# Column means of an 8192 x 8192 matrix: the last row group in loads of 4, 4, 2 and 1 blocks, five other blocks read at the start

## The chip, the cores and the metric

One core of a Trainium2 chip runs the program. The time is device microseconds of one execution, the median of five; less is better. A profile of one execution is at hand for the kernel before. Five engines work side by side, each with its own queue of instructions: TensorE (PE in the profile, its weight loads PEld), VectorE (DVE), ScalarE (ACT), GpSimd (POOL) and SyncE (SP). SyncE and ScalarE also issue DMA transfers (SPq and ACTq), and these run on 16 DMA engines.

## The reference

```python
def setup_inputs():
    return {
        "x": np.random.randn(8192, 8192).astype(np.float32),
    }

def reference(x: np.ndarray) -> np.ndarray:
    return np.mean(x, axis=0)
```

The input is 268.4 MB of float32, the output 32 KB. Every element of x has to be read once and added once.

## The kernel before

**Tiling.** The rows are cut into G = 64 groups of P = 128 rows, one row for each partition; group g is `rows(g)`, 4 MB. The columns are cut into 16 blocks of F = 512. The on-chip buffer `bufs` has six slots of one group each: four receive loads, slot 4 (`both`) holds the sum of two groups, slot 5 (`acc`) the running sum.

**Loads.** `load` (line 75) issues a transfer on SyncE's queue and appends it to `loads`. Every second one also waits for the landing of the loads seven and eight back. The order of the queue is the order of the program: `head` (blocks 0 to 3 of group 60, 768 KB), groups 0 to 3, groups 4 and 5, `ahead` (blocks 8 to 12 of group 63, 1 MB), then a loop over g from 6 to 52 with two groups, 8 MB, in each load, then groups 54 to 59 one by one, then group 60 without the blocks of `head`, 61, 62, and group 63 in three pieces: blocks 0 to 8, 12 to 14 and 14 to 16. (Ranges of blocks are given as in the code, without their upper end.) A load into a slot waits until VectorE has read what was there.

**Sums on VectorE.** `add` (line 95) is a VectorE addition. In the loop there are two for each load: the two new groups into `both`, then `both` into `acc`. Where an addition must wait for a load and for the one before, a no-op on ScalarE or GpSimd (line 98) waits for both and VectorE waits for the no-op; which of the two engines it is goes by the number of additions so far. Groups 54 to 59 are added to `acc` one by one, of group 60 only the blocks from 3 on, of group 61 only those from 5 on. GpSimd adds blocks 13 to 16 of group 62 (line 136).

**Sums on TensorE.** What is left over, and `acc` itself, is summed over the 128 partitions by matmuls with a 128 x 32 block of ones divided by 8192 (line 169). A matmul of one block goes to one of four quarters of the array (`tile_position=(0, 32 * q)`) and leaves its sum in 32 partitions of PSUM, so four of them run side by side. In float32 each matmul is two instructions in the trace. `plan` gives the order: what stands ahead in it holds up all that follows, since TensorE takes it in order. Blocks 0 to 12 go to three banks of four blocks each (`banks`), blocks 12 to 16 in pieces of W = 256 columns to two smaller tiles (`ends`).

**The end.** ScalarE copies bank 2 into `both` (line 183) and stores it (line 186, `s2`), after the landing of `loads[-3]`; then it copies banks 0 and 1 and the first small tile. VectorE copies the second small tile to `tail` (line 201). SyncE stores banks 0 and 1 together (`s01`), ScalarE blocks 12 to 14 (`s3`), SyncE blocks 14 to 16 last. `landed` (line 70) is a no-op on SyncE that waits for DMAs; three of them stand behind the last store. Then the program closes (line 239): SyncE waits for the last landings, and all engines meet.

```python
    for lo, loaded in [(3, 3), (5, 0)]:
        row = bufs[:, (g + 2) % 4, :]
        dma = load(row[:, loaded * F:], rows(g)[:, loaded * F:])
        add(acc[:, lo * F:], acc[:, lo * F:], row[:, lo * F:], [dma])
```

Of the kernel before, what the change touches and what calls it, by code (L numbers as in the profile page):

```python
# [8 lines left out]
@with_exitstack  # L9
def kernel(  # L10
    ctx: ExitStack,
    tc: tile.TileContext,
    x: bass.AP,
    out: bass.AP,
):

    nc = tc.nc
    f32 = mybir.dt.float32
    M, N = x.shape  # L40
    P = nc.NUM_PARTITIONS
    F = 512
    W = F // 2
    WHOLE = 12
    G = M // P
    U = 6
    sync = mybir.DependencyInfo(mybir.DependencyClass.Sync, mybir.DependencyReason.DATA)

    sb = ctx.enter_context(tc.tile_pool(name="sb", bufs=1))
    psp = ctx.enter_context(tc.tile_pool(name="psum", bufs=1, space=bass.MemoryType.PSUM))  # L50

    bufs = sb.tile([P, U, N], f32, name="bufs")
    both = bufs[:, U - 2, :]
    acc = bufs[:, U - 1, :]
    ones = sb.tile([P, 32], f32, name="ones")
    ahead = sb.tile([P, 4 * F], f32, name="ahead")
    tail = sb.tile([P, W], f32, name="tail")
    warm = sb.tile([P, 32], f32, name="warm")
    nc.gpsimd.memset(ones[:], 1.0 / M)  # L59
    ready = sb.tile([P, 1], f32, name="ready")  # L60
    tc.keep_in_program_order(
        nc.gpsimd.tensor_add(out=ready[:], in0=ones[:, 0:1], in1=ones[:, 1:2]))  # L62
    banks = [psp.tile([P, F], f32, name=f"bank{b}") for b in range(3)]
    ends = [psp.tile([P, W], f32, name=f"end{e}") for e in range(2)]

    loads = []

    def landed(*inss):

        nop = tc.keep_in_program_order(nc.sync.nop()).ins  # L70
        for o in inss:
            tc.add_manual_dep(nop, o.name, sync, reason="SyncE waits")

    def load(dst, src):
        ins = tc.keep_in_program_order(nc.sync.dma_start(out=dst, in_=src)).ins  # L75
        k = len(loads)
        over = loads[k - 8:k - 6] if k >= 8 and k % 2 == 0 else []
        tc.declare_no_dep(ins, group="loads", keep=over, reason="the reader of the buffer waited")
        for o in over:
            tc.add_manual_dep(ins, o.name, sync, reason="covers the next load too")  # L80
        tc.add_to_no_dep_group("loads", ins)
        loads.append(ins)
        return ins

    def rows(g, n=1):
        return x[g * P:(g + n) * P, :]

    def load_rows(g, u, n):
        return load(bufs[:, u:u + n, :], rows(g, n).rearrange("(p j) c -> p j c", j=n))

    adds, joins = [], {}

    def add(dst, a, b, dmas):

        ins = nc.vector.tensor_add(out=dst, in0=a, in1=b).ins  # L95
        if dmas and adds:
            waiter = nc.scalar if len(adds) % 8 > 1 else nc.gpsimd
            nop = joins[waiter] = tc.keep_in_program_order(waiter.nop()).ins  # L98
            for o in dmas + adds[-1:]:
                tc.add_manual_dep(nop, o.name, sync, reason="the no-op waits")  # L100
            for group in ("loads", "adds"):
                tc.declare_no_dep(ins, group=group, reason="the no-op waited")
            tc.add_manual_dep(ins, nop.name, sync, reason="waits for both at once")
        elif adds:
            tc.declare_no_dep(ins, group="loads", reason="the add ahead waited")
        tc.add_to_no_dep_group("adds", ins)
        adds.append(ins)

    head = sb.tile([P, 3 * F], f32, name="head")
    load(head[:], rows(G - 4)[:, :3 * F])  # L110
    first, second = load_rows(0, 0, 4), load_rows(4, 4, 2)
    load(ahead[:], rows(G - 1)[:, 8 * F:WHOLE * F])
    add(bufs[:, 2:4, :], bufs[:, 2:4, :], bufs[:, 0:2, :], [first])
    add(bufs[:, 4:6, :], bufs[:, 4:6, :], bufs[:, 2:4, :], [second])
    add(acc, acc, both, [])
    tc.keep_in_program_order(nc.scalar.copy(out=warm[:], in_=ones[:]))  # L116
    g = 6
    while g < G - 10:
        u = (g + 2) % 4
        dma = load_rows(g, u, 2)  # L120
        add(both, bufs[:, u, :], bufs[:, u + 1, :], [dma])
        add(acc, acc, both, [])
        g += 2

    while g < G - 4:
        row = bufs[:, (g + 2) % 4, :]
        add(acc, acc, row, [load(row, rows(g))])
        g += 1
    for lo, loaded in [(3, 3), (5, 0)]:
        row = bufs[:, (g + 2) % 4, :]  # L130
        dma = load(row[:, loaded * F:], rows(g)[:, loaded * F:])
        add(acc[:, lo * F:], acc[:, lo * F:], row[:, lo * F:], [dma])
        g += 1
    r61, r62, r63 = [bufs[:, (g + 1 + j) % 4, :] for j in range(3)]
    load(r62, rows(g))
    tc.keep_in_program_order(nc.gpsimd.tensor_add(  # L136
        out=acc[:, 13 * F:], in0=acc[:, 13 * F:], in1=r62[:, 13 * F:]))
    g += 1
    for lo, hi in [(0, 8), (12, 14), (14, 16)]:
        load(r63[:, lo * F:hi * F], rows(g)[:, lo * F:hi * F])  # L140

    plan = [
        (ahead, 8, 12),
        (acc, 3, 5),
        (acc, 0, 3),
        (r61, 0, 5),
        (head, 0, 3),
        (acc, 5, 12),
        (r62, 0, 12),
        (r62, 12, 13),  # L150
        (acc, 12, 14),
        (acc, 14, 16),
        (r63, 0, 8),
        (r63, 12, 14),
        (r63, 14, 16),
    ]
    sums = []
    for row, lo, hi in plan:
        base = 8 * F if row is ahead else 0
        if lo < WHOLE:  # L160
            for i in range(lo, hi):
                cols = row[:, i * F - base:(i + 1) * F - base]
                sums.append((banks[i // 4], i % 4, cols))
        else:
            for c in range(lo * F, hi * F, W):
                e, q = divmod(c // W - 2 * WHOLE, 4)
                sums.append((ends[e], q, row[:, c:c + W]))
    for n, (dst, q, cols) in enumerate(sums):
        tc.keep_in_program_order(nc.tensor.matmul(  # L169
            out=dst[32 * q:32 * q + 32, :],  # L170
            lhsT=ones[:],
            rhs=cols,
            start=all(d is not dst or k != q for d, k, _ in sums[:n]),
            stop=all(d is not dst or k != q for d, k, _ in sums[n + 1:]),
            tile_position=(0, 32 * q),
            skip_group_check=True,
        ))

    res = both[:, :3 * F].rearrange("p (b c) -> p b c", b=3)
    tails = [both[:, 3 * F:3 * F + W], tail[:]]  # L180

    def copy(dst, src):
        tc.keep_in_program_order(nc.scalar.copy(out=dst, in_=src))  # L183

    def store(engine, dst, src, *then):
        ins = tc.keep_in_program_order(engine.dma_start(out=dst, in_=src)).ins
        for o in then:
            tc.add_manual_dep(ins, o.name, sync, reason="follows that load")
        return ins

    def end(e):
        return (out[(WHOLE + 2 * e) * F:(WHOLE + 2 * e + 2) * F].rearrange("(q c) -> q c", q=4),
                tails[e][0:P:32, :])

    copy(res[:, 2, :], banks[2][:])
    s2 = store(nc.scalar, out[8 * F:12 * F].rearrange("(q c) -> q c", q=4), res[0:P:32, 2, :],
               loads[-3])
    for b in range(2):
        copy(res[:, b, :], banks[b][:])
    copy(tails[0], ends[0][:])  # L200
    nc.vector.tensor_copy(out=tails[1], in_=ends[1][:])  # L201
    landed(*loads[-8:-6])
    landed(*loads[-6:-4])
    landed(*loads[-4:-2])
    landed(*joins.values())
    s01 = store(nc.sync, out[:8 * F].rearrange("(b q c) -> q b c", b=2, q=4), res[0:P:32, 0:2, :])
    s3 = store(nc.scalar, *end(0))
    store(nc.sync, *end(1))
    landed(loads[-2], s2)
    landed(loads[-1], adds[-1])  # L210
    landed(s01, s3)
    hold = tc.keep_in_program_order(nc.vector.nop()).ins
    tc.add_manual_dep(hold, s01.name, sync, reason="VectorE ends late")


# [28 lines left out]
```

## Time and profile before

| | before |
|---|---|
| median of 5 runs | 628.49 us (628.31 to 628.56) |
| the profiled execution, and its span | 628.49 us, 626.57 us |
| VectorE busy | 526.1 us, 60 instructions |
| TensorE busy | 17.6 us, 124 instructions |
| GpSimd busy | 4.0 us, 7 instructions |
| an addition of 128 x 8192 on VectorE | 8.69 us |
| a matmul instruction of 512 columns, of 256 | 592 ns, 380 ns (medians); the first ones 1061 ns |
| a copy of 128 x 512, 128 x 256 on ScalarE | 585 ns, 378 ns |
| the copy of 128 x 256 on VectorE (`tail`) | 424 ns |

The span runs from the first instruction to the last; 1.9 us of the device time lie around it. Times in the profile are counted from the start of the span. In a line of the timeline the first number is the start, the second the length, then come the engine, the line of the program, the operation, what it writes and reads, and in brackets how long the engine had been idle and what ended that. In the chain of waits the two numbers are start and length of each piece of the chain that ended last, followed back from the end.

### The profile page before, as it was taken

What the parts mean: (1) busy time and instruction counts of PE and PEld (TensorE: products, weight loads), DVE (VectorE), ACT (ScalarE), POOL (GpSimd) and SP (SyncE); (2) the same over time, 40 slices, a digit from 0 to 9 for tenths busy, and PEclk for the clock granted to TensorE, in tenths of its full rate; (3) what the DMA queues carried; (4) which work ended last, traced back from release to release, by engine and by line L of the source; (5) the groups of instructions that cost most, each with busy time, mean ns of one, the idle gap of its engine ahead of it and who ended that gap; (6) DMA issues with size and microseconds to landing.
All of it is one profiled execution on the core that took longest, in us unless ns stands there. A gap on an engine that the chain in (4) does not pass through costs nothing.

```text
span 626.6 us, 475 instructions
## 1 busy us (share of the span) xinstructions
PE 17.6 (3%) x124; PEld 5.0 (1%) x124; DVE 526.1 (84%) x60; ACT 3.5 (1%) x6; POOL 4.0 (1%) x7
## 2 busy tenths in 40 slices
PE   0000100000000000000000000000000000000027
PEld 0000000000000000000000000000000000000002
DVE  0028999999888998888988889888898888999991
ACT  0000000000000000000000000000000000000001
POOL 0000000000000000000000000000000000000002
PEclk9999999999999999999999999999999999999999
DMA  9999999999999999999999999999999999999997
GB/s 385 469 402 413 457 469 402 448 423 427 443 410 460 406 464 402 469 402 469 402 469 402 469 402 469 402 469 402 452 418 427 443 410 429 433 435 435 423 433 303
DMA packets 5926, 268.50 MB, mean 429 GB/s; under 512 B 656, under 2 KB 664, under 8 KB 1060
## 3 DMA queue, kind: packets, MB, share of 16 engines
q1 hardware_dynamic: 5908, 268.46, 99.2%
q8 instruction: 1, 0.02, 0.0%
q10 hardware_dynamic: 16, 0.01, 0.0%
q14 instruction: 1, 0.01, 0.0%
HBM read 268.44 MB, written 0.03 MB: 428 GB/s over the span
## 4 chain that ended last, share of the span: by engine, by line
DMA 56%; DVE 33%; another core or an unknown queue 10%; issue 0%; SPq 0%; PE 0%; ACTq 0%; POOLq 0%; POOL 0%
DMA bufs<-in_x_dram 56%; DVE bufs L95 33%; SPq L75 0%; PE end L169 0%; ACTq L98 0%; DVE tail L201 0%; POOLq L98 0%; POOL ready L62 0%; POOL ones L59 0%; POOLq L228 0%
## 5 line engine op out<-in xcount | busy, mean ns | idle before, releaser
L95 DVE TENSOR_TENSOR bufs<-bufs 128x8192 f32<-128x8192 f32 (+3 forms) x59 | 525.6, 8909 | 87.8 <-DMA bufs<-in_x_dram 43.7
L169 PE MATMUL bank<-bufs,ones 128*32 128x512 f32 x74 | 12.6, 706 | 540.3 <-DVE bufs L95 539.8
L201 DVE COPY tail<-end 128x256 f32<-128x256 f32 x1 | 0.4, 424 | 10.2 <-PE end L169 10.2
L169 PEld LDWEIGHTS bank<-bufs,ones 128*32 128x32 f32 x74 | 3.0, 120 | 549.6 <-DVE bufs L95 541.8
L136 POOL TENSOR_TENSOR bufs<-bufs 128x1536 f32<-128x1536 f32 x1 | 3.5, 3473 | 614.5 <-DMA bufs<-in_x_dram 614.5
L183 ACT COPY bufs<-bank 128x512 f32<-128x512 f32 x3 | 1.8, 585 | 619.0 <-PE bank L169 619.0
L169 PE MATMUL bank<-ahead,ones 128*32 128x512 f32 x8 | 1.9, 1057 | 65.6 <-DMA ahead<-in_x_dram 65.6
L169 PE MATMUL end<-bufs,ones 128*32 128x256 f32 x36 | 3.3, 385 | 0.1
L169 PE MATMUL bank<-head,ones 128*32 128x512 f32 x6 | 1.9, 600 | 0.0
L169 PEld LDWEIGHTS end<-bufs,ones 128*32 128x32 f32 x36 | 1.4, 109 | 2.4 <-DMA bufs<-in_x_dram 0.8
L116 ACT ACT_TABLE_LOAD x1 | 1.3, 1283 | 0.7 <-PEq L228 0.7
L169 PEld LDWEIGHTS bank<-ahead,ones 128*32 128x32 f32 x8 | 0.2, 138 | 65.5 <-issue 65.5
L183 ACT COPY bufs<-end 128x256 f32<-128x256 f32 x1 | 0.4, 378 | 0.0
L169 PEld LDWEIGHTS bank<-head,ones 128*32 128x32 f32 x6 | 0.4, 108 | 0.6 <-issue 0.6
L116 ACT COPY warm<-ones 128x32 f32<-128x32 f32 x1 | 0.2, 218 | 0.0
L62 POOL TENSOR_TENSOR ready<-ones 128x1 f32<-128x1 f32 x1 | 0.2, 192 | 0.1
L59 POOL MEMSET ones<- 128x32 f32 x1 | 0.1, 124 | 0.3 <-POOLq L228 0.3
L228 POOL MEMSET const-bfloat16-1.0<- 128x1 bf16 x1 | 0.1, 101 | 0.0
L228 POOL MEMSET const-uint8-127<- 128x1 uint8 x1 | 0.1, 101 | 0.0
L228 POOL MEMSET const-float32-0.0<- 128x1 f32 x1 | 0.1, 98 | 0.2 <-issue 0.2
L228 POOL MEMSET const-float32-1.0<- 128x1 f32 x1 | 0.1, 98 | 0.0
## 6 DMA issues: line engine op xcount, KB each, us to landing
bufs<-in_x_dram SPq DMA_DIRECT2D x8, 4096.0 KB, 24.1
bufs<-in_x_dram SPq DMA_DIRECT2D x1, 3328.0 KB
bufs<-in_x_dram SPq DMA_DIRECT2D x1, 2048.0 KB, 20.3
ahead<-in_x_dram SPq DMA_DIRECT2D x1, 1024.0 KB
bufs<-in_x_dram SPq DMA_DIRECT2D x2, 512.0 KB, 21.5
head<-in_x_dram SPq DMA_DIRECT2D x1, 768.0 KB
bufs<-in_x_dram SPq DMA_DIRECT2D x26, 29.9
out_dram<-bufs ACTq DMA_DIRECT2D x1, 8.0 KB
```

The lines of the kernel that those rows point to most:

```text
L59: nc.gpsimd.memset(ones[:], 1.0 / M)
L62: nc.gpsimd.tensor_add(out=ready[:], in0=ones[:, 0:1], in1=ones[:, 1:2]))
L95: ins = nc.vector.tensor_add(out=dst, in0=a, in1=b).ins
L116: tc.keep_in_program_order(nc.scalar.copy(out=warm[:], in_=ones[:]))
L136: tc.keep_in_program_order(nc.gpsimd.tensor_add(out=acc[:, 13 * F:], in0=acc[:, 13 * F:], in1=r62[:, 13 * F:]))
L169: tc.keep_in_program_order(nc.tensor.matmul(out=dst[32 * q:32 * q + 32, :], lhsT=ones[:], rhs=cols, start=all(d is not dst or k != q for d ...
L183: tc.keep_in_program_order(nc.scalar.copy(out=dst, in_=src))
L201: nc.vector.tensor_copy(out=tails[1], in_=ends[1][:])
L228: nc = _bacc.Bacc("TRN2", target_bir_lowering=False, num_devices=1)
```

## The change

Four things are changed together.

1. What is read at the start: instead of `head` and `ahead` there is one tile, `early`, of seven blocks. Blocks 14 to 16 of group 60 are read first of all, blocks 9 to 14 of group 63 behind groups 4 and 5. TensorE no longer sums them; GpSimd adds them to `acc` in the loop, four blocks behind the iteration g = 24 and three behind g = 32, and the next addition to `acc` on VectorE waits for that.
2. Group 60 is loaded and added as blocks 0 to 14. Group 63 is read in four pieces: blocks 4 to 8, 0 to 4, 14 to 16, and 8 to 9.
3. GpSimd adds blocks 14 to 16 and then block 8 of group 62 to `acc`, as two instructions.
4. On TensorE, blocks 0 to 8 go to two banks as before; blocks 9 to 14, 14 to 16 and 8 to 9 are spread over the four quarters in tiles `wide`, `two` and `last`, by a new function `spread`. Matmuls of block 8 of `acc` stand behind those of blocks 0 to 4 of group 63. There are five stores in place of four: blocks 9 to 14 (ScalarE), 4 to 8 and 0 to 4 (SyncE), 14 to 16 (ScalarE), 8 to 9 (SyncE).

```diff
-    W = F // 2
-    WHOLE = 12
+    W = F // 4
...
-    ahead = sb.tile([P, 4 * F], f32, name="ahead")
+    early = sb.tile([P, 7 * F], f32, name="early")
...
-    banks = [psp.tile([P, F], f32, name=f"bank{b}") for b in range(3)]
-    ends = [psp.tile([P, W], f32, name=f"end{e}") for e in range(2)]
+    banks = [psp.tile([P, F], f32, name=f"bank{b}") for b in range(2)]
+    wide = psp.tile([P, 2 * F], f32, name="wide")
+    two = psp.tile([P, 2 * W], f32, name="two")
+    last = psp.tile([P, W], f32, name="last")
...
-    head = sb.tile([P, 3 * F], f32, name="head")
-    load(head[:], rows(G - 4)[:, :3 * F])
+    load(early[:, 5 * F:], rows(G - 4)[:, 14 * F:])
     first, second = load_rows(0, 0, 4), load_rows(4, 4, 2)
-    load(ahead[:], rows(G - 1)[:, 8 * F:WHOLE * F])
+    load(early[:, :5 * F], rows(G - 1)[:, 9 * F:14 * F])
...
         add(both, bufs[:, u, :], bufs[:, u + 1, :], [dma])
-        add(acc, acc, both, [])
+        add(acc, acc, both, ahead)
+        ahead = []
+        if g in (24, 32):
+            lo, hi = (0, 4) if g == 24 else (4, 7)
+            cols = slice((9 + lo) * F, (9 + hi) * F)
+            ins = tc.keep_in_program_order(nc.gpsimd.tensor_add(
+                out=acc[:, cols], in0=acc[:, cols], in1=early[:, lo * F:hi * F])).ins
+            tc.add_to_no_dep_group("early", ins)
+            ahead = [ins]
         g += 2
...
-    for lo, loaded in [(3, 3), (5, 0)]:
+    for lo, hi, loaded in [(0, 14, 14), (5, 16, 16)]:
         row = bufs[:, (g + 2) % 4, :]
-        dma = load(row[:, loaded * F:], rows(g)[:, loaded * F:])
-        add(acc[:, lo * F:], acc[:, lo * F:], row[:, lo * F:], [dma])
+        dma = load(row[:, :loaded * F], rows(g)[:, :loaded * F])
+        cols = slice(lo * F, hi * F)
+        add(acc[:, cols], acc[:, cols], row[:, cols], [dma])
         g += 1
...
-    tc.keep_in_program_order(nc.gpsimd.tensor_add(
-        out=acc[:, 13 * F:], in0=acc[:, 13 * F:], in1=r62[:, 13 * F:]))
+    for cols in [slice(14 * F, 16 * F), slice(8 * F, 9 * F)]:
+        tc.keep_in_program_order(nc.gpsimd.tensor_add(
+            out=acc[:, cols], in0=acc[:, cols], in1=r62[:, cols]))
     g += 1
-    for lo, hi in [(0, 8), (12, 14), (14, 16)]:
+    for lo, hi in [(4, 8), (0, 4), (14, 16), (8, 9)]:
         load(r63[:, lo * F:hi * F], rows(g)[:, lo * F:hi * F])
...
+    def blocks(row, lo, hi):
+        for i in range(lo, hi):
+            sums.append((banks[i // 4], i % 4, 0, row[:, i * F:(i + 1) * F]))
+
+    def spread(dst, row, lo, hi):
+        n = (hi - lo) * W
+        for c in range(0, n, F):
+            for q in range(4):
+                at = lo * F + q * n + c
+                sums.append((dst, q, c, row[:, at:at + min(F, n - c)]))
+
+    blocks(acc, 2, 5)
+    blocks(acc, 0, 2)
+    blocks(r61, 0, 5)
+    blocks(acc, 5, 8)
+    spread(wide, acc, 9, 14)
+    blocks(r62, 0, 8)
+    spread(wide, r62, 9, 14)
+    blocks(r63, 4, 8)
+    spread(two, acc, 14, 16)
+    blocks(r63, 0, 4)
+    spread(last, acc, 8, 9)
+    spread(two, r63, 14, 16)
+    spread(last, r63, 8, 9)
...
+    copy(res5, wide[:, :5 * W])
+    s5 = store(nc.scalar, part(9, 14), res5[0:P:32, :], loads[-4])
+    copy(res[:, 1, :], banks[1][:])
+    copy(res[:, 0, :], banks[0][:])
+    copy(res2, two[:])
+    nc.vector.tensor_copy(out=tail[:], in_=last[:])
     landed(*loads[-8:-6])
     landed(*loads[-6:-4])
     landed(*loads[-4:-2])
     landed(*joins.values())
...
+    s1 = store(nc.sync, part(4, 8), res[0:P:32, 1, :])
+    s0 = store(nc.sync, part(0, 4), res[0:P:32, 0, :])
+    s2 = store(nc.scalar, part(14, 16), res2[0:P:32, :])
+    store(nc.sync, part(8, 9), tail[0:P:32, :])
+    landed(loads[-2], s5)
     landed(loads[-1], adds[-1])
-    landed(s01, s3)
+    landed(s0, s1)
+    landed(s2)
     hold = tc.keep_in_program_order(nc.vector.nop()).ins
-    tc.add_manual_dep(hold, s01.name, sync, reason="VectorE ends late")
+    tc.add_manual_dep(hold, s0.name, sync, reason="VectorE ends late")
```

## The prediction

> **What bounds the kernel now.** I read the page first: the DMA row by slices, then busy time.
>
> ```profile
> span 626.6 us, 475 instructions
> ...
> DMA  9999999999999999999999999999999999999997
> ...
> HBM read 268.44 MB, written 0.03 MB: 428 GB/s over the span
> ```
>
> The DMA engines are full in every slice but the last. The 268.44 MB are x itself, and the change reads the same bytes, so only the order of the stream and what follows its last byte can move the time. Next, the chain of waits, in the loop and at the end:
>
> ```profile
> 491.19 8.70 DVE bufs L95
> 499.89 0.02 issue
> 499.91 29.92 DMA bufs<-in_x_dram
> ...
> 600.94 21.93 DMA bufs<-in_x_dram
> 622.88 0.04 issue
> 622.92 0.68 PE end L169 x8
> 623.60 0.02 issue
> 623.62 0.42 DVE tail L201
> ```
>
> In the loop this pattern returns every 38.70 us (461.21 to 499.91), two 8 MB loads, so 19.35 a load. A load lands 29.92 after its issue: 10.6 us (29.92 - 19.35) it stands behind the one before. VectorE (2 x 8.70 + 0.04 = 17.4) has 1.9 us over per load. After 622.88 there is a tail of 3.7 us. Third, the timeline of the end:
>
> ```profile
> 607.32 0.21 PEld L169 LDWEIGHTS bank<-bufs,ones 128*32 128x32 f32 x8 [541.57 <-DVE bufs L95]
> ...
> 608.18 0.18 PEld L169 LDWEIGHTS bank<-bufs,ones 128*32 128x32 f32 x1 [0.65 <-issue]
> ...
> 612.25 0.14 PEld L169 LDWEIGHTS bank<-head,ones 128*32 128x32 f32 x4
> ...
> 612.67 0.11 PEld L169 LDWEIGHTS bank<-head,ones 128*32 128x32 f32 x1 [0.28 <-issue]
> ...
> 615.60 3.47 POOL L136 TENSOR_TENSOR bufs<-bufs 128x1536 f32<-128x1536 f32 x1 [614.47 <-DMA bufs<-in_x_dram]
> ...
> 620.44 1.08 ACTq L186 DMA_DIRECT2D out_dram<-bufs  x1
> ...
> 622.94 0.38 ACT L183 COPY bufs<-end 128x256 f32<-128x256 f32 x1
> 623.07 0.71 SPq L186 DMA_DIRECT2D out_dram<-bufs  x1
> 623.35 0.52 ACTq L186 DMA_DIRECT2D out_dram<-bufs  x1
> 623.62 0.42 DVE L201 COPY tail<-end 128x256 f32<-128x256 f32 x1 [10.23 <-PE end L169]
> 624.08 0.56 SPq L186 DMA_DIRECT2D out_dram<-tail  x1
> ```
>
> Two stores run side by side at the end: ScalarE's from 623.35 and SyncE's last from 624.08. By the semaphore times they land at 625.24 (1.88 after the issue began) and 625.72 (1.64). SyncE meets the first at 625.25, needs two more waits and a branch, and would be at its last wait at about 625.60; the last store holds it to 625.735. From there closing takes 0.83, to 626.57. So the last store leads ScalarE's by only **0.13 us**: that is the room for a gain before the other store takes over.
>
> **The loads.** Each load is 128 packets, eight for each DMA engine. By the packet records they take (median) 160 ns at 4 KB, 234 at 6 KB, 309 at 8 KB, 615 at 16 KB, 992 at 26 KB, 1218 at 32 KB; a 2 KB one, from a store, 86. Removed per engine: 8 x (234 head + 309 ahead + 992 row 60 + 615 + 160 + 160) = 19.76 us. Added: 8 x (160 and 386 early + 1067 row 60 + 309 + 309 + 160 + 86) = 19.82, with 386 for 10 KB and 1067 for 28 KB between their neighbours. The stream is **0.06 later**. A 2 KB load packet has no row: between half a 4 KB one (80, -0.05 us) and a whole one (160, +0.6). I take the store's 86, since size alone sets the others. Landings counted back from 622.94 (row group 63 named by its blocks, 4-8, 0-4, 14-16, 8-9): 14-16 at 622.25, 0-4 at 620.97, 4-8 at 618.5, row 62 at 616.0. The two 512 KB loads of before landed 1.28 and 1.25 apart.
>
> The Trainium skill speaks against small loads: "DMA: Bandwidth & Descriptors", "Rules for kernel authors", wants at least 1 MiB a DMA, and "Anatomy of one DMA" gives each one (fitted on another issuing path) some 2.0 us of fixed cost. By an estimate from that page, paid one after the other, the extra load would bring 630.4; the landings 1.25 apart say that it overlaps, and I go by them.
>
> SyncE issues one load more by 601.4 (0.43 each from 600.09). Its wait on loads eight back asks for row 59, landed at 588.1. Nothing starves: the last one issued lands 21.9 later.
>
> **GpSimd in the loop.** Two adds, 4 blocks after g=24 and 3 after g=32: 3.47 x 4/3 = 4.63 and 3.47 us. The first starts at 276.45, when VectorE's second add ends and 1.85 us before its next. No row shows both engines adding at once. Bounds: no slowing (0), or all of it serial (VectorE 4.63 late). I take 4.63 - 1.85 = 2.8 late, the early starter first. The next load is issued that much later, against 10.6 us of cover, and VectorE wins back 1.9 a load, with ten loads left after g=32. Both bounds cost **0**. Uncovered, the price would be the excess over 10.6. The new no-op stands on GpSimd's queue behind that add; behind it wait VectorE's second add and the later no-op for g=28, which waits for a landing 20 us away anyway.
>
> The skill's "SBUF — State Buffer", "two separate sides", says that the two engines lock a shared port pair for a whole instruction. No run here shows it; it would give the same zero.
>
> **VectorE at the end.** Row 60's add grows from 6656 to 7168 columns, at (8.69 - 7.09)/1536 = 1.04 ns each: 0.53. It starts at 600.17 as before, since VectorE is behind its loads there, and row 61's ends at 613.92, not 613.39. Row 62 lands at 616.0: hidden, with 2 us to spare.
>
> **TensorE.** Ahead's four blocks and head's three go. The first ten blocks start 0.53 later, at 607.85. Block 0 of each four shares one quarter of the array, and that quarter gets 4 blocks, 8 instructions, as before. Before, they came 0.857 apart until about 612.1 and 0.43 afterwards. I take the switch at the same 4.8 us after the start, 612.65. Eight blocks of acc take 2 x 0.43 + 2 x 0.43 + 2 x 0.11 = 1.9 (to 615.9), row 62's 13 blocks 2.8 (616.05 to 618.85), 4-8 0.86 (619.7), acc's two 0.43, 0-4 0.86 (621.0 to 621.9), acc's one 0.21, 14-16 0.43 (622.3 to 622.7). All are done before the last landing, with 0.2 to spare. GpSimd's two adds, 2.36 and 1.25 (3.47 by columns, plus 0.1 for a second start), end at 618.5 and 619.8, ahead of need at 619.7 and 621.9.
>
> **The last block.** Eight instructions of 128 columns in place of 256. 512 columns take 592 ns, 256 take 380: 0.83 a column, so 274. With the first start 0.045 after landing, the second four 0.11 later (0.21 for 256) and the same 0.045 spread, TensorE ends at 623.40. VectorE's copy goes from 0.42 to 0.42 - 128 x 1.04 ns = 0.29: 623.47 to 623.76. The store is issued at 623.79 and lands 1.64 later, **625.43**: 0.29 ahead of before. A 128-column matmul has no row: at worst its second four keeps 0.21 (+0.1), at best it gains a bit more (-0.05).
>
> **The other stores.** ScalarE: 640 columns 0.69 (619.0 to 619.7), its store 1.08 (to 620.8), bank 1 (to 621.4), bank 0 from 622.15 (1.15 after landing, as 620.45 to 621.60) to 622.75, then blocks 14-16: landing 622.25 + 0.68 TensorE + 0.11, so 623.04 to 623.42. Store at 623.45, landing at **625.33**, 0.09 later than ScalarE's before. SyncE's two (0.55 each; bound 1.08, the issue inside the stream) run 621.45 to 622.0 and 622.78 to 623.33, free by 623.79. The wait for ScalarE's store now stands last: 625.34, branch 0.07, 0.17, 0.05, last wait at about 625.63, past the final store's 625.43. The gain is 625.735 - 625.63 = 0.1, and **the store of blocks 14-16 becomes the end**.
>
> **The sum.** The profiled execution took 628.49, 1.9 outside its 626.57 span, and 628.49 is also the median of the runs. 628.49 - 0.1 gives **628.4**, with -0.3 (only the last store counts) to +0.6 (2 KB packets) about it.
>
> **Rivals.**
> A. No gain or a small loss: 628.5 to 629.1, at 628.7. ScalarE's store lands later, by its queue or by 2 KB packets at 4 KB's time. For it: a 0.1 margin, and ScalarE's store of before took 1.08 inside the stream. Against: 0.7 of slack on ScalarE ahead of 622.15.
> B. Slower: TensorE stays at the 0.857 pace. Without head's blocks it runs dry before acc is ready at 613.95; if the fast pace comes only 4.8 us into that stretch (618.75), acc's blocks end at 617.8, row 62's at 621.1, 4-8 at 622.0, 0-4 at 623.2 and the last near 624.3 (+0.9), and ScalarE, still paying 1.08 for its first store at 622, ends 1.2 late: 629.6. It decides (over 629.75) if the fast pace comes after about 619.2. Against: the ten blocks keep one quarter busy for up to 8 x 0.857 = 6.9 us, and before the pace rose after 4.8 with that quarter alone at work.
> C. The diff doesn't reach the end: GpSimd's adds stall the loop by more than 10.6 us, and each us over it is lost whole, 629.4 for 11.6. Against: 4.63 is all there is to wait for.
> D. Shorter than I say: ScalarE's last copy and store overlap better, the last store alone decides: 628.2.
>
> **How the numbers follow.** Forecast (628.2 to 628.6) 0.58, A 0.22, B 0.09, C 0.03, D 0.08. Time 628.4. The range 628.1 to 629.1 holds the forecast, D and A. A measurement tells about 0.2% (1.26 us) from no change: faster means below 627.23, which only an unseen gain reaches (0.02); slower above 629.75, a third of B, half of C and what I have not seen (0.06); the rest is 0.92.
>
> **What would show it.** DMA full to the last slice and the last landing near 622.9; no later issue of loads after 276 or 354 than the one in flight covers; TensorE at 0.43 from 614 on; the 128-column copy near 0.29; the last two stores landing within 0.2 us of each other. Wrong if the stream ends over 0.3 later, if the 0.857 pace shows past 615, or if a store other than those two ends last.

## The result, and the profile after

The changed kernel takes 630.37 us in the median of 24 runs (628.33 to 630.70), the kernel before 628.55 in 44 runs (628.31 to 628.98). The ratio is 1.0023, with a 95% interval of 1.0017 to 1.0029: a loss of 1.8 us by the medians and of 1.4 us by the ratio, where 0.1 us of gain was forecast, and outside the range of 628.1 to 629.1. The runs of the changed kernel lie in two groups, with nothing between: five at 628.33 to 628.72, inside the range of the forecast, and nineteen at 629.94 to 630.70. The median lies in the upper group, the ratio mixes both. The profiled execution (630.15 us, span 628.4) belongs to the second, and what it shows is that group's story.

From the page of the changed kernel, the span, the DMA row by slices and the queues:

```profile
span 628.4 us, 481 instructions
...
DMA  9999999999999999999999999999999999999996
...
q1 hardware_dynamic: 6056, 268.46, 98.9%
q8 instruction: 1, 0.02, 0.0%
...
q14 instruction: 1, 0.01, 0.0%
HBM read 268.44 MB, written 0.03 MB: 427 GB/s over the span
```

The loads still fill every slice but the last, so GpSimd's additions in the loop starve nothing. The two rows called "instruction" (packets, MB, share) stand on the page of before too, with the same numbers. They look like nothing: one packet of 16 KB, one of 8 KB, 0.0% of the DMA engines' time. They turn out to be the cause.

The chain of waits of the changed kernel, at the end (start, length, what):

```profile
601.13 0.43 SPq L76
601.56 0.04 issue
601.60 22.88 DMA bufs<-in_x_dram
624.48 0.04 issue
624.52 0.47 PE last L181 x8
624.99 0.02 issue
625.02 0.29 DVE tail L212
```

It has the shape of before: last landing, eight matmul instructions, a copy, a store. What stands behind the landing is as short as planned. The landing itself is at 624.48, where the forecast had 622.94. The timeline of the same stretch:

```profile
622.38 0.58 ACT L196 COPY bufs<-bank 128x512 f32<-128x512 f32 x1 [0.55 <-PE bank L181]
622.52 0.16 PEld L181 LDWEIGHTS two<-bufs,ones 128*32 128x32 f32 x8 [0.26 <-DMA bufs<-in_x_dram]
622.52 0.64 PE L181 MATMUL two<-bufs,ones 128*32 128x256 f32 x8
623.23 0.37 ACT L196 COPY bufs<-two 128x256 f32<-128x256 f32 x1 [0.26 <-PE two L181]
623.63 0.52 ACTq L199 DMA_DIRECT2D out_dram<-bufs  x1
624.52 0.16 PEld L181 LDWEIGHTS last<-bufs,ones 128*32 128x32 f32 x8 [1.84 <-DMA bufs<-in_x_dram]
624.52 0.43 PE L181 MATMUL last<-bufs,ones 128*32 128x128 f32 x8 [1.36 <-DMA bufs<-in_x_dram]
625.02 0.29 DVE L212 COPY tail<-last 128x128 f32<-128x128 f32 x1 [10.90 <-PE last L181]
625.34 0.50 SPq L199 DMA_DIRECT2D out_dram<-tail  x1
```

The bracket on the `last` matmuls is the thing to see: TensorE stood idle for 1.36 us, and a DMA ended that. The matmuls of blocks 14 to 16 began at 622.52, those of block 8 only 2.00 us later, though their load of 256 KB was planned 0.7 us behind. TensorE, VectorE and SyncE were all waiting for one transfer.

A load raises its semaphore 16 times, once for each DMA engine. From the semaphore records of the last load:

```
blocks 14 to 16:  16 increments from 621.90 to 622.48
block 8:          15 increments from 622.55 to 623.09, the last one at 624.48
```

Fifteen engines were in time and one was 1.39 us behind them. The packet records say what it was doing:

```
start    end      queue  bytes  ns
622.312  623.398  8      16384  1086    a read of instructions
623.382  623.614  1       2048   232    the last two packets of the
623.599  623.827  1       2048   228    load of block 8
         622.633  1       2048    84    latest end of any other load packet
```

One engine took up a 16 KB read of instructions for 1.09 us while two packets of the last load still stood behind it. In before the read is there as well, at 622.20 to 623.27; but the last load packet of the engine that took it had already ended, and all 16 increments of the last landing came between 622.41 and 622.88.

The final store is hit too. It was issued at 625.34, and its four rows land at 626.91, 626.92, 626.92 and 627.52. The 8 KB read of queue 14 runs from 626.17 to 626.52, and the packet of the fourth row begins right behind it, at 626.56. In before this read comes at 626.23, behind the last landing at 625.72; here the store meets it. Of the 0.60 only 0.05 lies in the start of that packet; the rest comes between packet and semaphore, where no record shows anything. That the read is the cause is read from three traces that agree (here, after_plus16 and after_hold: the fourth row 0.60 to 0.86 late, its packet at the end of the read); in none of the other fourteen traces is a row of the last store so late. No run here moves that read alone. So the span grows against the forecast by 1.54 (landing) and 0.60 (one row of the store), less some 0.2, because the store of blocks 14 to 16 is no longer the end: 1.9, and 626.57 - 0.1 + 1.9 = 628.4, as measured.

### The profile page after: what moved, and what is told of

It reads as the page before. It is cut to its first block, busy times and chain, and to the rows that moved or that the text cites. A ratio compares the mean times of both kernels' runs of the same rounds, so it can differ in the third digit from the quotient of the medians.

```text
span 628.4 us, 481 instructions
## 1 busy us (share of the span) xinstructions
PE 14.2 (2%) x122; PEld 4.2 (1%) x122; DVE 530.4 (84%) x60; ACT 3.7 (1%) x6; POOL 12.1 (2%) x10
## 4 chain that ended last, share of the span: by engine, by line
DMA 55%; DVE 34%; another core or an unknown queue 10%; issue 0%; SPq 0%; ACTq 0%; PE 0%; POOL 0%; POOLq 0%
DMA bufs<-in_x_dram 55%; DVE bufs L96 34%; SPq L76 0%; ACTq L99 0%; PE last L181 0%; POOLq L99 0%; DVE tail L212 0%; POOL ready L61 0%; POOL ones L58 0%; POOLq L241 0%
## 5 line engine op out<-in xcount | busy, mean ns | idle before, releaser
L181 PE MATMUL bank<-bufs,ones 128*32 128x512 f32 x58 | 10.6, 728 | 609.4 <-DVE bufs L96 608.7
L129 POOL TENSOR_TENSOR bufs<-bufs,early 128x2048 f32<-128x2048 f32 (+1 forms) x2 | 7.9, 3954 | 348.4 <-DVE bufs L96 348.4
L148 POOL TENSOR_TENSOR bufs<-bufs 128x1024 f32<-128x1024 f32 (+1 forms) x2 | 3.6, 1834 | 258.9 <-DMA bufs<-in_x_dram 258.9
L181 PE MATMUL wide<-bufs,ones 128*32 128x512 f32 (+1 forms) x32 | 3.4, 433 | 0.0
L181 PEld LDWEIGHTS wide<-bufs,ones 128*32 128x32 f32 x32 | 1.3, 110 | 2.3 <-issue 2.3
L181 PE MATMUL two<-bufs,ones 128*32 128x256 f32 x16 | 1.3, 385 | 0.0
```

Source lines behind the costliest of these rows:

```text
L129: ins = tc.keep_in_program_order(nc.gpsimd.tensor_add(out=acc[:, cols], in0=acc[:, cols], in1=early[:, lo * F:hi * F])).ins
L148: tc.keep_in_program_order(nc.gpsimd.tensor_add(out=acc[:, cols], in0=acc[:, cols], in1=r62[:, cols]))
L181: tc.keep_in_program_order(nc.tensor.matmul(out=dst[32 * q:32 * q + 32, c:c + cols.shape[1]], lhsT=ones[:], rhs=cols, start=all((d is dst, ...
```

## The experiments

Three theories stood at the start. **Theory 1**: the read of instructions, ahead of one engine's last load packets, is the whole loss. **Theory 2**: the 2 KB packets of the last load are slow in themselves. **Theory 3**: the stores that now run inside the stream delay its end. (Theories 2 and 3 are called rivals 2 and 3 in the expectations.) Every kernel ran beside the kernel before, which had medians of 628.54 to 628.66. The times:

```
kernel              median (range), runs           ratio [95%]             read   last two landings
after_minus32       628.33 (628.08-628.58), 11     0.9984 [0.9959,1.001]   622.84  622.84, 623.48
after_last_two      630.37 (629.0-630.57), 11      1.0022 [1.0013,1.0031]  622.64  622.11, 624.79
after_stores_late   630.31 (629.78-630.64), 8      1.0026 [1.0016,1.0037]  622.32  622.81, 623.41
before_plus16       629.80 (629.55-630.16), 11     1.0019 [1.0011,1.0028]  619.00  622.95, 624.17
after_plus16        630.70 (630.17-630.9), 6       1.0031 [1.0019,1.0043]  622.82  622.96, 624.98
after_plus64        630.31 (628.19-630.62), 12     1.0019 [1.0011,1.0028]  622.23  622.39, 623.02
after_plus208       629.58 (629.36-630.27), 11     1.0016 [1.0008,1.0025]    6.26  623.64, 624.28
after_tail16        630.12 (628.2-630.55), 11      1.0013 [1.0004,1.0022]  622.22  622.53, 623.15
after_tail64        630.39 (628.22-631.1), 11      1.0022 [1.0013,1.0031]  622.34  622.56, 623.18
before_split        628.56 (628.45-628.94), 11     0.9999 [0.999,1.0008]   622.41  621.85, 623.12
after_join          629.24 (629.13-629.61), 11     1.0010 [1.0001,1.0019]  622.23  622.43, 623.04
after_vector62      629.28 (629.13-629.6), 11      1.0011 [1.0002,1.0019]  623.63  623.27, 623.88
vector62_hold       629.28 (629.06-629.49), 11     1.0011 [1.0002,1.002]   623.04  623.30, 623.92
after_vector8       629.73 (629.46-631.16), 11     1.0022 [1.0013,1.0031]  623.29  623.10, 623.72
after_hold          630.44 (630.12-630.97), 6      1.0031 [1.0019,1.0042]  622.89  623.06, 625.05
```

"Read" is the start of the 16 KB read in the kernel's profiled execution. That execution lies in the lower group for after_plus64, after_tail16 and after_tail64, and at the low end of its runs for after_stores_late; so its landings there are not those of the median.

### Without the read ahead of the last packets

TensorE's sums of blocks 9 to 14 of row group 62 are left out, which is work of the kernel: 32 of its instructions fewer.

```diff
     blocks(r62, 0, 8)
-    spread(wide, r62, 9, 14)
     blocks(r63, 4, 8)
```

> The changed kernel without the sums of blocks 9 to 14 of row group 62 on TensorE: 8 matmuls, 32 TensorE instructions fewer. Theory 1 (in the changed kernel a 16 KB read of instructions for TensorE, at 622.3, holds one of the 16 DMA engines for 1.09 us ahead of its last load packets; it comes at a fixed place of TensorE's instructions): with 32 fewer in front of it that read starts after the last load packet (after 622.6) or not at all, the last load lands about 0.7 after the one before it, and the time is 628.2 to 628.6 in nearly all runs. Rival 2 (a last load of 256 KB in 2 KB packets lands late by itself): the last load still lands 2 us after the one before, 630.2 to 630.5. Rival 3 (stores issued inside the load stream hold it up): also 630.2 to 630.5.

628.33 us, and all 11 runs in one group. From the chain of waits of this kernel:

```profile
601.06 20.50 DMA bufs<-in_x_dram
621.56 0.04 issue
621.60 1.06 PE bank L180 x8
622.67 0.22 PE last L180 x8
622.89 0.63 PE two L180 x8
623.52 0.00 issue
623.52 0.47 PE last L180 x8
624.00 0.02 issue
624.02 0.29 DVE tail L211
```

The last wait for a DMA is no longer the one for block 8: it landed at 623.48, 0.64 behind blocks 14 to 16, while TensorE still had those in work (until 623.52). The read came at 622.84, 0.18 before the last load packet of all engines ended (0.32 in the changed kernel), and no load packet waited behind it; the final store landed at 625.93, ahead of its 8 KB read at 626.17. The last load is the same here, in the same 2 KB packets, and the same stores run in the stream. So the 2 us are not in them.

### The last two loads exchanged

```diff
-    for lo, hi in [(4, 8), (0, 4), (14, 16), (8, 9)]:
+    for lo, hi in [(4, 8), (0, 4), (8, 9), (14, 16)]:
```

TensorE's order follows. The load of 4 KB packets is then the last one.

> The changed kernel with the last two loads exchanged: block 8 first, then blocks 14 to 16, so that the last load has 4 KB packets. Theory 1: the read of instructions starts near 622.3 as before, ahead of the end of the stream, and the last load still lands 1 us or more late in most runs: 630 to 631. Rival 2: the last load lands at 622.9 as in the kernel before; with 0.4 more behind it (256 columns, copy on ScalarE) 628.5 to 629.0. Rival 3: as theory 1.

630.37, with the last landing 2.68 behind the one before, where 512 KB take 1.25. One increment is 1.45 behind the other fifteen, and the read at 622.64 stands ahead of it, as in the changed kernel. Three of the eleven runs are at 629.00 to 629.14, the rest at 630.26 to 630.57. The loss does not go with the 2 KB packets. Theory 2 falls.

### The stores behind the last landing

```diff
-    s5 = store(nc.scalar, part(9, 14), res5[0:P:32, :], loads[-4])
...
+    s5 = store(nc.scalar, part(9, 14), res5[0:P:32, :], loads[-1])
...
+    landed(loads[-2], loads[-1])
     s1 = store(nc.sync, part(4, 8), res[0:P:32, 1, :])
```

> The changed kernel with its two stores that were issued inside the load stream (blocks 9 to 14 and 4 to 8) behind the landing of the last load. Theory 1: the last load still lands about 2 us after the one before in most runs; the time is 630.3 to 631.5. Rival 2: the same. Rival 3: the last load lands 0.7 after the one before, and the time falls to 628.5 to 629.3, the stores behind it costing up to 0.8.

630.31: taking the stores of blocks 9 to 14 and 4 to 8 out of the stream gains nothing that can be told. This run alone does not decide on theory 3. The profiled execution is the lowest of this kernel's runs (629.78); its last two landings are 0.61 apart, as theory 3 expected, and what makes it long are the late stores themselves: ScalarE issues its two one after the other (1.92 from 623.64), and that of blocks 14 to 16 lands last, at 626.83, where it lands at 625.14 to 625.32 in the profiled executions of after_plus64, after_tail16 and after_tail64. For the median there is no trace. Theory 3 falls by other runs: after_minus32 has the same stores inside the stream and its landings in order, and so have those three; the kernel of the next section has the loss without these stores.

### The read made to come earlier, in the kernel before

Four matmuls on blocks of `ahead`, 16 instructions, into a spare tile; the rest is the kernel before.

```diff
+    for q in range(4):
+        tc.keep_in_program_order(nc.tensor.matmul(
+            out=spare[32 * q:32 * q + 32, :], lhsT=ones[:],
+            rhs=ahead[:, q * F:(q + 1) * F], start=True, stop=True,
+            tile_position=(0, 32 * q), skip_group_check=True))
```

> The kernel before with four more matmuls (16 TensorE instructions) of the early tile at about 65 us, into a PSUM tile that nothing reads. They cost nothing where they stand. Theory 1: the read of instructions comes 16 TensorE instructions earlier, so about 0.4 to 0.9 us earlier than its 622.2, inside the stream of loads; one DMA engine's last packets come up to 1.1 us later and the time is 629.3 to 630.0 in most runs. Rivals 2 and 3: loads and stores are those of before, 628.5.

629.80, a loss of 1.2 without any part of the change. The read moved from 622.20 to 619.00, into the stream, by more than the 0.4 to 0.9 expected. (The granted clock was 0.57 in seven of the eleven runs and 1.0 in four; these take 629.70 to 629.94 and 629.55 to 630.16, so the loss does not go with the clock.) From the chain of waits of this kernel:

```profile
600.04 21.66 DMA bufs<-in_x_dram
621.70 0.14 issue
621.84 1.92 PE bank L180 x16
623.76 0.43 PE end L180 x8
624.20 0.02 issue
624.22 0.68 PE end L180 x8
624.92 0.42 DVE tail L212
```

Blocks 0 to 8 land at 621.70, 1.4 later than in before (620.35), and all that follows keeps that distance. The spread of the 16 increments is 0.30 in the landing at 615.37 and 1.74, 1.70 and 1.66 in the three behind the read, of which 1.4 is one engine alone. **An engine that was held once does not catch up**: by these landings, each engine has its own share of every load and works it off in order, and the others do not take any of it over.

### More instructions on TensorE, at the start and at the end

Matmuls on `ones` into a spare tile, ahead of all sums (4, 16 or 52 of them: 16, 64 or 208 instructions) or behind them (4 or 16: 16 or 64).

```diff
+    for k in range(16):
+        q = k % 4
+        tc.keep_in_program_order(nc.tensor.matmul(
+            out=spare[32 * q:32 * q + 32, :], lhsT=ones[:], rhs=ones[:],
+            start=True, stop=True, tile_position=(0, 32 * q), skip_group_check=True))
```

> The changed kernel with 4 small matmuls more (16 TensorE instructions) on the ones tile at the start, into a PSUM tile that nothing reads. Theory 1: the read of instructions comes earlier than 622.3, well inside the stream, so every run is hit: 629.6 to 630.4 with no run under 629. One DMA engine lands about 1.1 late in every load from there on. Rivals: the same loads and stores as the changed kernel, so its mix of runs, a fifth of them under 628.8.

> The same with 16 small matmuls, 64 TensorE instructions. Theory 1 with engines that each work off their own share: the read comes some us earlier still, and the engine that it held stays behind to the end, 629.6 to 630.2. Theory 1 with a stream that evens such a delay out: below 629 once the read is several us ahead of the end.

> The same with 52 small matmuls, 208 TensorE instructions, so that the read of instructions comes in the first 20 us or at the first real matmul at 608. If the engine stays behind for 600 us: 629.5 to 630.2. If the loads even it out: 628.2 to 628.6, as the changed kernel was forecast.

> The changed kernel with 16 small matmuls (64 TensorE instructions) behind its last one, on the ones tile, into a PSUM tile that nothing reads; same output. The read of instructions at 622.3 did not move when 16 or 64 instructions stood in front. Theory 1a: it is asked for when TensorE's sequencer has run ahead to the end of its program, so it hangs on how many instructions are left; with 64 more left it comes after the last load has landed, and every run is at 628.2 to 628.8. Theory 1b: it hangs on the place from the start: no change, 630.2 to 630.5 in four runs of five.

> The same with 4 small matmuls, 16 TensorE instructions, behind the last one. Theory 1a: the read comes later by up to 0.4 us, and most runs fall to 628.2 to 628.8. Theory 1b: 630.2 to 630.5 in four runs of five.

16 or 64 more, at either end, leave the read between 622.2 and 622.9 and the time in the same two groups (the six runs of after_plus16 all in the upper one). So the earlier read expected of after_plus16 and after_plus64 did not come, and theory 1a fails with after_tail16 and after_tail64: that the number of TensorE's instructions alone sets when the read comes is refuted, though 208 more did move it, and 32 fewer by some 0.15 against the end of the stream. In after_plus16 the final store is hit as well: three rows at 627.40 to 627.41, the fourth at 628.04, with the 8 KB read at 626.70.

With 208 more the read goes to 6.26, into the first loads. The spread of the increments, landing by landing, from the semaphore records:

```
                4 us   44 us   65 us   200 us   500 us   last
before          0.47   0.47    0.48    0.48     0.47     0.47
after_minus32   0.37   0.26    0.23    0.24     0.25     0.23
after_plus208   0.59   1.82    1.67    1.51     1.51     1.45
```

The read took 0.94 us of one engine at 6.26 us. The last increment is 1.56 behind the ninth at 44 us and still 1.24 at 624 us (0.31 in the first landing, before the read took effect). The loss of 0.9 to 1.0 us is paid at the end, six hundred microseconds after its cause. It is smaller than the changed kernel's (629.36 and 630.15 in the profiled executions), since the last landing comes at 624.28 in place of 624.48, and mainly since the store stays clear of the 8 KB read (landed at 626.72, read at 627.03).

### The number of loads

The loads of blocks 0 to 8 in two pieces in the kernel before, and in one piece in the changed kernel:

```diff
-    for lo, hi in [(0, 8), (12, 14), (14, 16)]:
+    for lo, hi in [(4, 8), (0, 4), (12, 14), (14, 16)]:
```
```diff
-    for lo, hi in [(4, 8), (0, 4), (14, 16), (8, 9)]:
+    for lo, hi in [(0, 8), (14, 16), (8, 9)]:
```

> The kernel before with its load of blocks 0 to 8 of the last row group split in two (4 to 8, then 0 to 4): 41 loads as in the changed kernel, the rest as before. Theory 1: what counts is when TensorE gets on in its instructions against the end of the stream. TensorE now sums blocks 4 to 8 1.2 us earlier, so it reaches the last instructions earlier (0.8 instead of 0.3 us ahead of the last packet): most runs 629.6 to 630.3. If the number of TensorE instructions or the smaller last load is what counts: 628.5.

> The changed kernel with blocks 0 to 8 of the last row group in one load, as before: 40 loads; the rest as in the change. Theory 1: TensorE gets the blocks 4 to 8 2.4 us later, so its last instructions are reached after the stream has ended: all runs at 628.5 to 629.0 (TensorE's queue ahead of the last block costs up to 0.4). If the small last load or the stores are what counts: 630.2 to 630.8.

One more load costs the kernel before nothing (ratio 0.9999), so it is not the count of 41 loads. The 629.6 to 630.3 that theory 1 expected of it did not come either: TensorE had blocks 4 to 8 earlier, but the read did not move forward (622.41, in before 622.20). After_join is spared by the read as well: its last landings are 0.62 apart. It takes 629.24, over the 628.5 to 629.0 expected, for another reason, seen in its chain of waits:

```profile
621.28 1.06 PE bank L181 x8
622.34 0.43 PE two L181 x8
622.77 0.86 PE bank L181 x8
623.63 0.22 PE last L181 x8
623.85 0.43 PE two L181 x8
624.28 0.25 PE last L181 x8
624.56 0.29 DVE tail L212
```

With eight blocks landing at once, TensorE runs without a gap from 621.28 and reaches the last block 1.2 us after it landed (623.04).

### Versions that might be faster

VectorE adds blocks 8 to 16 of row group 62 in three instructions, in place of GpSimd's two and of TensorE's 32; SyncE stores blocks 9 to 14. In a second version a no-op on GpSimd waits for a store, so that GpSimd does not end early; the third has the three additions in one.

```diff
-    for cols in [slice(14 * F, 16 * F), slice(8 * F, 9 * F)]:
-        tc.keep_in_program_order(nc.gpsimd.tensor_add(
+    for cols in [slice(9 * F, 14 * F), slice(14 * F, 16 * F), slice(8 * F, 9 * F)]:
+        tc.keep_in_program_order(nc.vector.tensor_add(
...
-    spread(wide, r62, 9, 14)
```

> The changed kernel, same output, with VectorE (idle from 614) adding blocks 9 to 14, 14 to 16 and 8 of row group 62 to acc in place of GpSimd and TensorE: 32 TensorE instructions fewer, TensorE sums blocks 9 to 14 once, behind blocks 4 to 8 of group 63; the store of blocks 9 to 14 goes to SyncE's queue. Theory 1: the 16 KB read of instructions starts after the last load packet, the last load lands 0.7 after the one before, 628.1 to 628.6 in nearly all runs, 1.8 less than the changed kernel. Rivals (small last load, stores in the stream): they keep 630.2 to 630.5.

> The kernel in which VectorE adds row group 62, with one more no-op: GpSimd waits for the store of blocks 0 to 4 before its program ends. Without it GpSimd had ended at 600.4, and an 8 KB read of instructions at 619.9 held one DMA engine for 0.7 us and left its loads 0.8 late to the end. Theory 1 (any read of instructions inside the stream leaves one engine behind to the end) with GpSimd's early end as its cause: the read moves behind the last load, and all runs are at 628.2 to 628.6, faster than both kernels. If that read has another cause: 629.1 to 629.6 as without the no-op.

> The changed kernel with the same no-op on GpSimd. If the 16 KB read at 622.3 is asked for when GpSimd's program ends, at 620.1: it moves behind the last load, all runs at 628.2 to 628.7. If it belongs to TensorE: no change, 630.2 to 630.5 in four runs of five, since GpSimd's end at 620 asks for nothing that is served before the stream ends.

> The changed kernel with blocks 8 to 16 of row group 62 added by VectorE in one instruction (in place of GpSimd's two and of TensorE's 32 instructions on blocks 9 to 14); blocks 9 to 14 are stored by SyncE. The output is the reference's. It is the version of three VectorE additions (629.28) with two instructions fewer on VectorE. Theory 1, that only reads of instructions ahead of an engine's last load packets cost time, and that the 8 KB read at 619.9 came with VectorE's three additions: no 8 KB read ahead of 623, the 16 KB read behind the stream as without TensorE's 32 instructions, last landing near 622.9 to 623.2, and 628.2 to 628.6. Rival: the 8 KB read comes whatever the number of VectorE's instructions, one DMA engine is 0.8 late from 620 on, and the time is 629.1 to 629.5. Third: the 16 KB read falls ahead of the last load packets again: 630.0 to 630.6.

As theory 1 had it, with 32 instructions fewer on TensorE the 16 KB read comes late in all three (623.04 to 623.63) and holds up no load packet. But now the 8 KB read comes early: at 619.93, 619.96 and 619.77. In after_vector62 an 8 KB load packet that began as the read ended took 968 ns in place of 313, and from then on the spread of the landings is 1.3 to 1.4 in place of 0.59; one engine is 0.77 behind the other fifteen at the last one. The time, 629.28, is 0.6 to 0.7 above the kernel before beside it, and 0.7 to 1.2 above the 628.1 to 628.6 expected. GpSimd's end does not ask for this read (the no-op changed nothing, 629.28 again), nor for the 16 KB one (after_hold stays at 630.44, read at 622.89), and VectorE's number of instructions does not either: with one addition the read is still at 619.77. That misses the 628.2 to 628.6 expected; the single addition also holds back TensorE's sums of `wide` until 621.04, and the time is 629.73.

No version with the whole sum was faster than the kernel before by more than the noise.

## Why the prediction was wrong

**The step that failed** is "The loads", and in it "The stream is 0.06 later" with block 8 landing at 622.94. Its bytes and packets were right: the loads of blocks 4 to 8, 0 to 4 and 14 to 16 land at 618.71, 621.21 and 622.48, each 0.21 to 0.24 after the forecast, and a 2 KB load packet takes 84 to 86 ns where 86 was taken. (That was partly luck: the twelve 2 KB store packets of before took 84 to 158 ns, 101.5 in the median.) What failed was the assumption that the 16 engines carry nothing but the loads up to the last byte. A 16 KB read of instructions held one of them for 1.09 us, and the last load landed at 624.48, 1.54 later than forecast; fifteen of its sixteen engines were there by 623.09. None of the four rivals had this mechanism, and the row that would have suggested it ("q8 instruction") stood on the page of before and was read past, its share being 0.0%. The right question to such a row is not its share but when it comes: in before it began 0.16 us ahead of the end of the last load packet (622.36).

The margin that decides is two packets of 2 KB. In the profiled executions of after_plus64, after_tail16 and after_tail64 the read starts at 622.22 to 622.34, as in the changed kernel (622.31), and finds no load packet left behind it; they take 628.19 to 628.30. Against the end of the stream the read comes no later there: it starts 0.33 to 0.48 before the last load packet of all engines ends, in the changed kernel 0.32. What differs is how far the one engine that takes it has come. The 16 increments of a load lie apart even where no read holds an engine: in the last load but one by 0.58 to 0.88 in the four traces where the read then met load packets of the last load (after, after_plus16, after_hold, after_last_two), by 0.26 to 0.55 in those where it met none, but for after_stores_late with 0.71. No run tests whether this spread decides. By the traces, the lower group of the runs is the runs in which the read meets no load packet. That this holds for each single run of the changed kernel was not seen, as only one has a trace.

**The rest, by its steps.** Without the read the forecast's time comes out: after_minus32 and the lower groups of the changed kernel, after_plus64, after_tail16 and after_tail64 show 628.1 to 628.8 for 628.4.

- *GpSimd in the loop.* The additions take 4.49 and 3.42 (4.63 and 3.47 forecast). From the timeline and the chain of waits of the changed kernel:

```profile
276.66 4.49 POOL L129 TENSOR_TENSOR bufs<-bufs,early 128x2048 f32<-128x2048 f32 x1 [275.53 <-DVE bufs L96]
```
```profile
248.53 29.92 DMA bufs<-in_x_dram
...
278.51 11.20 DVE bufs L96
...
289.77 8.70 DVE bufs L96
...
307.29 29.21 DMA bufs<-in_x_dram
```

  VectorE's addition takes 11.20 in place of 8.70: 2.5 late, 2.8 forecast. The next chain piece on the DMA is 0.7 shorter and no more: the cover of 10.6 swallows the rest, and the cost is zero, as forecast.
- *GpSimd's last blocks.* 2.38 and 1.29 us, 2.36 and 1.25 forecast; both are ready ahead of need.
- *TensorE.* The quicker pace came at 612.1 (612.65 forecast), and it never ran dry at the slower one: rival B had no part. Rival C neither.
- *The last block.* 0.51 from its landing to TensorE's end and 278 ns an instruction (0.46 and 274 forecast), the copy 0.29 (0.29).
- *The other stores.* ScalarE's copy of 640 columns 0.69 (0.69), its store 1.07 (1.08), the copies of banks 1 and 0 at 621.25 and 622.38, the store of blocks 14 to 16 issued at 623.63 and landed at 625.24 (623.45 and 625.33). That it would be the end could not show here, since the last store came 2.3 us behind it. Where the read held nothing, it was not the end: in after_plus64, after_tail16 and after_tail64 the last store lands 0.33 to 0.34 behind the one of blocks 14 to 16, where 0.10 was forecast, and the span ends 0.86 to 0.88 after it, as in before (0.85). So the last store alone decided, as in rival D, which gives 628.2; their 628.19 to 628.30 agree.
- *The final store.* Issue to landing 2.18, where 1.64 was forecast; to its third row, which the 8 KB read does not precede, it is 1.58 (626.92). It is 1.59 in after_minus32.

What the forecast called a test of itself, "Wrong if the stream ends over 0.3 later", is what happened.

**Shown and not shown.** Shown: the late landing comes from the read's place, by a kernel in which no load packet stands behind it (628.33, all 11 runs) and by the kernel before with the read moved into the stream (629.80). Argued, from three traces: the further 0.60 of the final store, by the 8 KB read. Not settled: what asks for the read, and when. It is not GpSimd's end, nor TensorE's number of instructions by any rule that fits all the kernels (in the changed kernel 208 more moved it and 32 fewer a little, 16 and 64 more didn't; 16 more moved it in the kernel before), nor the number of loads. What brings the 8 KB read forward to 619.9 in the three versions with VectorE is open too.

The Trainium skill, "Runtime: NRT & Kernel Launch", section "Instruction fetch mechanics", says that each engine's sequencer refills its instruction memory through a DMA queue of its own, in blocks of 16 KiB, and calls the cost of it mostly hidden. The size agrees with the 16,384 bytes of the record. "Mostly hidden" holds in the kernel before, where no load packet stands behind the read. It does not hold where some do: a stream that is full to its end pays 0.9 to 1.2 us for one block (after_plus208 and before_plus16), and the measurement decides.

## What to carry to other kernels

In a kernel that is bound by its DMA engines and has little else in its tail, ask when each small transfer of the page comes, not only how long it is: a packet of 0.0% that one of 16 engines takes up shortly before its last packets, or anywhere in a stream without gaps, is paid at the end. Read the last landing engine by engine, by its 16 increments: one late increment among fifteen in time is a held engine, not a slow load. A change of the instruction streams, even of an engine far from the critical path, can move such a read, so a gain of 0.1 us worked out from the stream alone is not safe against it.

## What the runs showed of the hardware

- A 16 KB read of instructions took one DMA engine 0.93 to 1.44 us, most often 1.03 to 1.10, where a 16 KB load packet took 615 ns. Two 2 KB load packets directly behind it took 232 and 228 ns in place of 84 in the changed kernel (about the same in after_plus16 and after_hold).
- The lag of an engine that was held once persisted through 600 us of full streaming (after_plus208: increments 1.82 apart at 44 us, 1.45 at 624; 0.47 throughout in before).
- GpSimd's addition of 128 x 2048 made VectorE's addition beside it 2.50 us longer, and itself took no longer than its columns ask (4.49 for 4.63). The two began 1.85 apart, and 276.66 + 4.49 = 281.15 is 2.64 behind VectorE's start at 278.51: within 0.14 us, VectorE lost as much time as GpSimd's instruction ran beside it. The second pair agrees: 1.57 side by side (354.06 + 3.42 - 355.91), and VectorE's addition 10.11, 1.41 longer. This is the bound "all of it serial" of the forecast.
